# Summing the adaLN scale and shift vectors along the free dimension, and starting the first feed-forward layer one contraction tile at a time

## The chip, the cores and the metric

One core of a Trainium2 chip runs the whole program. The metric is the device time of one execution in microseconds (us); lower is better. The engines named below: TensorE (PE in the profile; PEld is its weight loads), VectorE (DVE), ScalarE (ACT), GpSimd (POOL), and SyncE (SP), which issues the DMA transfers.

## The reference: what is computed

A two-layer encoder on one sequence of 256 positions, width 1024, everything in float32. Each layer has three sub-layers (a feed-forward one, a mixer, a feed-forward one); layer 0's mixer is a gated MLP, layer 1's is banded attention. Every sub-layer is modulated by one vector `c`:

```
c_act = silu(c)                                        # (1, 1024)
mod   = (c_act @ w_ada[l] + b_ada[l]).reshape(9, 1024) # shift, scale, gate of 3 sub-layers
h = x * (1 + scale[i]) + shift[i]
y = swiglu(h, ffn_gu, ffn_down)                        # (silu(h @ Wg) * (h @ Wu)) @ Wd, d_ff = 2816
x = layer_norm(ALPHA * x + 0.5 * (1 + gate[i]) * y, ln_g, ln_b)
```

The shared keys and values of layer 1 have a scale and a shift of their own (`w_ada_kv`). So there are 20 vectors of 1024 numbers that are each a product of `c_act` with a 1024x1024 matrix: 14 scales and shifts, and 6 gates.

## The kernel before, in words

The 256 positions are two tiles (t = 0, 1) of 128 partitions. A large product takes a modulated, transposed activation tile (features on partitions) as the stationary operand and 512 weight columns as the moving one. For precision each operand is split into a rounded part `hi` and a remainder `lo` (fp32r): a product is three matmuls, `hi*hi`, `hi*lo`, `lo*hi` (L240, L241, L243, in `mm_unit`). A weight "unit" is a 128x1024 piece (512 KB): SP loads it into one of 6 `raw` buffers, ACT casts it to `hi` (L196), DVE subtracts to get `lo` (L197), and PE runs 12 matmuls on it (2 position tiles x 2 accumulators x 3).

A modulation vector is summed in `ada_slice`. The matrix is read in 8 pieces in which partition p holds row 8p+j; DVE multiplies piece j by the per-partition number `c_act[:, j]` and adds it to an accumulator `acc` (L114). After 8 pieces the sum over the 128 partitions remains. For a scale or shift (`finish_cols`) PE transposes the accumulator in 8 blocks of 128x128 (L129) and DVE reduces each half along its free dimension (L130), which leaves the vector with features on partitions. For a gate (`finish_gate`) PE multiplies by a matrix of ones instead. The pieces are fed in between the weight units: `ada_phase` lists the vectors of a phase with a number of units over which to spread them, and `pump`, called once for each unit, issues the next piece when enough credit has built up.

The first feed-forward layer starts cold, in `first_gu_part`. Its first part is two chunks of gate/up columns (512 and 256 wide). Scale and shift are summed for the first 512 features (8 pieces, L438), then `x` for these features is transposed on PE (L458), modulated on ACT (L294) and split; then matmuls on contraction tiles 0 to 3 run while the second 512 features go the same way. In this region the order on SP and PE is as written; elsewhere a scheduler sets the order of each engine's instructions at build time. Every engine works through its own queue in order.

After the first part come a down projection of these 768 columns, and then the other four chunks of 512 and their down projection (`PARTS2`).

Of the kernel before, what the change touches and what calls it, by code (L numbers as in the profile page):

```python
# [8 lines left out]
F32 = mybir.dt.float32  # L9
# [5 lines left out]
P = 128  # L15
D = 1024
# [28 lines left out]


@with_exitstack
def encoder_kernel(ctx, tc, a, out):
# [11 lines left out]
    accp = pool("accp", 2)  # L60
# [14 lines left out]

    c_raw = const.tile([P, KD], F32, name="c_raw")
    nc.sync.dma_start(out=c_raw, in_=a["c"])
    X = [xp.tile([P, D], F32, name=f"X{t}") for t in range(NT)]
    c_act = const.tile([P, KD], F32, name="c_act")
    nc.scalar.activation(c_act, c_raw, AF.Silu)  # L80
    ident = const.tile([P, P], F32, name="ident")
    make_identity(nc, ident)
    ones = const.tile([P, P], F32, name="ones")
# [12 lines left out]

    def load_small():
        small_dma(lncols, a["lncols"])
# [5 lines left out]
    def ada_slice(key, w_src, b_src, finish):  # L104
        st = {"acc": None}
# [15 lines left out]

    def finish_cols(key):
        def f(acc):
            m = modp.tile([P, KD], F32, tag="mod", name=nm("mod"))
            for half in range(2):
                tp = pt.tile([P, 512], F32, tag="pt", name=nm("adt"))
                for q in range(4):
                    j = half * 4 + q
                    nc.tensor.transpose(tp[:, q * P:(q + 1) * P], acc[:, j * P:(j + 1) * P], ident)  # L129
                nc.vector.reduce_sum(m[:, half * 4:half * 4 + 4],  # L130
                                     tp.rearrange("p (q n) -> p q n", q=4), axis=AX.X)
            mods[key] = m
        return f
# [17 lines left out]
    def mk_slice(key):  # L151
        if key[0] == "kv":
            n0 = key[1] * D
            wv = a["w_ada_kv"].rearrange("(p j) n -> p j n", j=KD)[:, :, n0:n0 + D]
            return ada_slice(key, wv, a["b_ada_kv"][:, n0:n0 + D], finish_cols(key))
        l, m = key
        n0 = m * D
        wv = a["w_ada"][l].rearrange("(p j) n -> p j n", j=KD)[:, :, n0:n0 + D]
        fin = finish_gate(key, 1.0 if m == 5 else 0.5) if m % 3 == 2 else finish_cols(key)
        return ada_slice(key, wv, a["b_ada"][l:l + 1, n0:n0 + D], fin)  # L160
# [149 lines left out]
    def affine(scl, shift, ln):  # L310

        A = modp.tile([P, KD], F32, tag="A", name=nm("A"))
        B = modp.tile([P, KD], F32, tag="B", name=nm("B"))
        if ln is None:
            nc.vector.tensor_scalar(A, scl, 1.0, None, op0=ALU.add)
            nc.vector.tensor_copy(B, shift)
        else:
            g, b = lncols[:, 0, ln, :], lncols[:, 1, ln, :]
            nc.vector.scalar_tensor_tensor(A, scl, 1.0, g, op0=ALU.add, op1=ALU.mult)
            nc.vector.scalar_tensor_tensor(B, scl, 1.0, b, op0=ALU.add, op1=ALU.mult)  # L320
            nc.vector.tensor_tensor(B, B, shift, op=ALU.add)
        return A, B
# [91 lines left out]
    def first_gu_part(w_gu, part, aT):  # L414

        units = [gu_units(w_gu, c0, wd) for c0, wd in part]
        accs = []
        wv = a["w_ada"][0].rearrange("(p j) (m n) -> p j m n", j=KD, m=9)[:, :, 0:2, :]
        bv = a["b_ada"][0:1, :].rearrange("o (m n) -> o m n", m=9)[:, 0:2, :]

        chunks = [(0, 1), (1, 1), (2, 2), (4, 2), (6, 2)]

        HK = KD // 2
        CW = HK * P
        sums = []
        for c in range(2):
            acc = accp.tile([P, 2, CW], F32, tag="acc", name=nm("acc"))
            nc.gpsimd.memset(acc, 0.0)
            nc.gpsimd.memset(acc[32:33, 1, :], 1.0)
            sums.append(acc)  # L430

        def products(c, js):
            for j in js:
                raw = unitp.tile([P, 2, CW], F32, tag=("hi", "lo")[j % 2], name=nm("raw"))
                nc.sync.dma_start(out=raw, in_=wv[:, j, :, c * CW:(c + 1) * CW])
                if j == 0:
                    nc.sync.dma_start(out=sums[c][0:1], in_=bv[:, :, c * CW:(c + 1) * CW])
                nc.vector.scalar_tensor_tensor(sums[c], raw, c_act[:, j:j + 1], sums[c],  # L438
                                               op0=ALU.mult, op1=ALU.add)

        def load_x(c):
            for t in range(NT):
                nc.sync.dma_start(out=X[t][:, c * CW:(c + 1) * CW],
                                  in_=a["x"][t * P:(t + 1) * P, c * CW:(c + 1) * CW])

        def modulate(c):
            m8 = modp.tile([P, 2, HK], F32, tag="m8", name=nm("m8"))
            for m in range(2):
                tp = pt.tile([P, 512], F32, tag="pt", name=nm("adt"))
                for q in range(HK):  # L450
                    nc.tensor.transpose(tp[:, q * P:(q + 1) * P], sums[c][:, m, q * P:(q + 1) * P], ident)
                nc.vector.reduce_sum(m8[:, m], tp.rearrange("p (q n) -> p q n", q=HK), axis=AX.X)
            for t in range(NT):
                p, tag = (ps, "ps") if c == 0 else (pt, "pt")
                tp = p.tile([P, 512], F32, tag=tag, name=nm("hp"))
                for q in range(HK):
                    k = c * HK + q
                    nc.tensor.transpose(tp[:, q * P:(q + 1) * P], X[t][:, k * P:(k + 1) * P], ident)  # L458
                hT[t].extend(modulated(tp, m8[:, 1], m8[:, 0], range(HK), htp, "h"))

        def load_units(k):

            for gi, uis in ((0, (k, k + 1)), (1, (k // 2,))):
                for ui in uis:
                    get(units[gi], ui)

        def matmuls(*todo):
            for gi, ui in todo:
                for t in range(NT):
                    mm_unit(accs[gi][t], hT[t], units[gi][ui], ui, KD)  # L470

        products(0, range(KD))
        load_x(0)
        modulate(0)
        accs.extend([new_accs(wd // 256) for _ in range(NT)] for _, wd in part)
        load_units(0)
        products(1, range(KD // 2))
        matmuls((0, 0), (0, 1), (1, 0))
        load_units(2)
        products(1, range(KD // 2, KD))  # L480
        load_x(1)
        matmuls((0, 2), (0, 3))
        modulate(1)
        matmuls((1, 1))
        load_units(4)
        load_units(6)
        matmuls((0, 4), (0, 5), (1, 2), (0, 6), (0, 7), (1, 3))
        for gi, (c0, wd) in enumerate(part):
            for t in range(NT):
                gu_out(t, accs[gi][t], wd, aT)  # L490
# [348 lines left out]
```

## Time and profile before

| | us |
|---|---|
| median of 3 runs | 1082.26 (1081.93 to 1084.04) |
| profiled execution | 1084.99 |
| its span in the profile | 1083.2 |
| PE busy | 1038.2 |
| DVE busy | 872.8 |
| ACT busy | 520.5 |

The profile comes from one execution. The span is what the profiler saw of it, the rest lies around it. "Busy" is the time in which at least one instruction of the engine is in flight. A matmul's own duration is longer than the distance to the next one, since they are pipelined; a run of matmuls is therefore read by their starts. In a row of the timeline, "[18.14 <-DVE acc L438]" means that the engine had been idle for 18.14 us and that the DVE instruction of line 438 on `acc` released it.

### The profile page before, as it was taken

How to read it: one execution, taken by the hardware profiler on the slowest of the kernel's cores; microseconds unless marked ns; L12 is line 12 of the kernel's file. 1: busy time of each engine (PE TensorE's matmuls, PEld its weight loads, DVE VectorE, ACT ScalarE, POOL GpSimd, SP SyncE). 2: the span in 40 equal slices, each digit the busy share in tenths (PEclk: the TensorE clock that was granted, in tenths of full speed). 3: DMA queues.
4: the chain of work that ended last, by engine and by line, in shares of the span. 5: the costliest groups of instructions: out<-in, count | busy, mean ns of one | idle time of the engine just before them, and what ended most of it. 6: DMA issues, size and time to landing. Idle time of an engine off the chain costs nothing. (4 is left out here: it accounts for less than half of the span.)

```text
span 1083.2 us, 13718 instructions
## 1 busy us (share of the span) xinstructions
PE 1038.2 (96%) x4888; PEld 853.3 (79%) x4888; DVE 872.8 (81%) x1095; ACT 520.5 (48%) x732; POOL 38.6 (4%) x55
## 2 busy tenths in 40 slices
PE   2899999999999999999999999999999999999996
PEld 1678888878777787888887888887887788888886
DVE  5889885689999999988779997758998869645635
ACT  3445553374345464443439554343748656445530
POOL 1000000000000010000000000000000000000000
PEclk9999999999999999999999999999999999999999
DMA  8988988659788778999876798768698837745621
GB/s 281 356 296 318 328 314 303 214 180 306 258 284 315 258 265 302 336 339 312 323 241 206 264 336 281 244 215 277 217 346 306 291 92 253 258 157 168 241 78 40
DMA packets 111809, 281.55 MB, mean 260 GB/s; under 512 B 9574, under 2 KB 22118, under 8 KB 111740
## 3 DMA queue, kind: packets, MB, share of 16 engines
q1 hardware_dynamic: 111740, 280.67, 74.8%
q8 instruction: 38, 0.62, 0.2%
q14 instruction: 31, 0.25, 0.1%
HBM read 279.58 MB, written 1.05 MB: 259 GB/s over the span
## 5 line engine op out<-in xcount | busy, mean ns | idle before, releaser
L196 ACT CAST hi<-raw 128x1024 fp32r<-128x1024 f32 x344 | 357.6, 1057 | 268.8 <-DMA raw<-ffn_gu 96.4
L197 DVE TENSOR_TENSOR lo<-raw,hi 128x1024 fp32r<-128x1024 f32 x344 | 413.8, 1219 | 55.3 <-ACT hi L196 49.1
L240 PE MATMUL acc<-hi,hh 128*128 128x512 f32 x928 | 365.8, 397 | 3.9 <-ACT hh L275 3.0
L241 PE MATMUL acc<-lo,hh 128*128 128x512 f32 x928 | 361.0, 392 | 1.6 <-DVE lo L197 1.5
L243 PE MATMUL acc<-hi,hl 128*128 128x512 f32 x928 | 293.3, 391 | 0.0
L240 PEld LDWEIGHTS acc<-hi,hh 128*128 128x128 f32 x928 | 174.9, 189 | 40.9 <-ACT hh L275 4.4
L241 PEld LDWEIGHTS acc<-lo,hh 128*128 128x128 f32 x928 | 175.1, 189 | 37.5 <-DVE lo L197 3.2
L243 PEld LDWEIGHTS acc<-hi,hl 128*128 128x128 f32 x928 | 174.6, 188 | 36.8
L114 DVE SCALAR_TENSOR_TENSOR acc<-raw,c_act,acc 128x1024 f32<-128x1024 f32 x144 | 184.1, 1278 | 16.3 <-DMA raw<-w_ada 16.0
L240 PE MATMUL acc<-hi,th 128*128 128x512 f32 (+1 forms) x432 | 165.2, 388 | 0.5 <-ACT th L275 0.2
L241 PE MATMUL acc<-lo,th 128*128 128x512 f32 (+1 forms) x432 | 163.4, 384 | 1.0 <-DVE lo L197 0.9
L243 PE MATMUL acc<-hi,tl 128*128 128x512 f32 (+1 forms) x432 | 143.4, 383 | 0.0
L241 PEld LDWEIGHTS acc<-lo,th 128*128 128x128 f32 x432 | 80.9, 188 | 17.4 <-DVE lo L197 2.9
L240 PEld LDWEIGHTS acc<-hi,th 128*128 128x128 f32 x432 | 81.2, 188 | 16.3 <-ACT th L275 0.9
L243 PEld LDWEIGHTS acc<-hi,tl 128*128 128x128 f32 x432 | 80.5, 188 | 15.7
L403 ACT ACTIVATE sg<-acc 128x512 f32<-128x512 f32 (+1 forms) x48 | 27.1, 564 | 90.1 <-PE acc L243 89.6
L404 DVE TENSOR_TENSOR a<-acc,sg 128x512 f32<-128x512 f32 (+1 forms) x48 | 30.9, 643 | 47.9 <-ACT sg L403 47.9
L276 DVE TENSOR_TENSOR tl<-tp,th 128x512 fp32r<-128x512 f32 (+1 forms) x56 | 36.0, 648 | 38.3 <-ACT th L275 38.3
L275 ACT CAST th<-tp 128x512 fp32r<-128x512 f32 (+1 forms) x56 | 30.9, 556 | 73.3 <-PE tp L282 73.1
L294 ACT ACTIVATE hf<-hp,B,A 128x128 f32<-128x128 f32 x96 | 36.6, 474 | 58.7 <-PE hp L306 42.8
L334 DVE TENSOR_TENSOR gy<-acc,gate 128x512 f32<-128x512 f32 (+1 forms) x49 | 32.0, 673 | 17.8 <-PE acc L243 17.8
L110 POOL MEMSET acc<- 128x1024 f32 x18 | 17.2, 956 | 604.7 <-PE adt L129 429.2
(99 smaller groups left out, 593.6 us busy)
## 6 DMA issues: line engine op xcount, KB each, us to landing
raw<-ffn_gu SPq DMA_DIRECT2D x160, 512.0 KB, 5.9
raw<-w_ada SPq DMA_DIRECT2D x144, 512.0 KB, 5.1
raw<-ffn_down SPq DMA_DIRECT2D x88, 512.0 KB, 4.9
raw<-w_in SPq DMA_DIRECT2D x32, 512.0 KB, 6.0
raw<-ffn_gu SPq DMA_DIRECT2D x32, 256.0 KB, 4.7
raw<-w_out SPq DMA_DIRECT2D x16, 512.0 KB, 6.0
raw<-w_ada_kv SPq DMA_DIRECT2D x16, 512.0 KB, 5.2
raw<-w_kv SPq DMA_DIRECT2D x16, 512.0 KB, 5.7
```

The lines of the kernel that those rows point to most:

```text
L114: nc.vector.scalar_tensor_tensor(st["acc"], raw, c_act[:, j:j + 1], st["acc"], op0=ALU.mult, op1=ALU.add)
L196: nc.scalar.copy(hi, raw)
L197: last["lo"] = eng.tensor_tensor(lo, raw, hi.bitcast(F32), op=ALU.subtract)
L240: nc.tensor.matmul(acc, lhsT=xh, rhs=wh[:, sl], start=k == 0, stop=False)
L241: nc.tensor.matmul(acc, lhsT=xh, rhs=wl[:, sl], start=False, stop=False)
L243: nc.tensor.matmul(acc, lhsT=xl, rhs=wh[:, sl], start=False, stop=k == nk - 1)
L275: nc.scalar.copy(hi, src_ps)
L276: nc.vector.tensor_tensor(lo, src_ps, hi.bitcast(F32), op=ALU.subtract)
L294: nc.scalar.activation(hf[:, sl], tp[:, sl], AF.Identity, bias=B[:, j:j + 1], scale=A[:, j:j + 1])
L334: nc.vector.tensor_tensor(tmp, acc[:, :c1 - c0], g[:, sl], op=ALU.mult)
L403: nc.scalar.activation(sg[:, :wd], g, AF.Silu)
L404: nc.vector.tensor_tensor(av[:, :wd], u, sg[:, :wd], op=ALU.mult)
```

## The change

Three things change together.

1. The 14 scale and shift matrices are handed over transposed (`w_cols`, features in rows), 128 features a piece. `c_act` is spread over all partitions once (`c_row`), and one DVE instruction (`tensor_tensor_reduce`) multiplies a piece by it and sums along the free dimension, straight into the column of the result. The bias is its start value; 1 has been added to the biases of the scales, so that `affine` no longer adds it. PE's transposes and DVE's reductions of `finish_cols` go. Gates are summed as before, from `w_gate`, with one accumulator buffer in place of two.
2. The first part of the first feed-forward layer takes its first two chunks (512 and 512 columns) one contraction tile k at a time: 128 features of scale and of shift, `x` for these features (handed over transposed, `xT`), then one weight unit of each chunk. PE first runs 48 transposes of the identity into a tile that nothing reads. `x` itself is loaded later.
3. The first layer's parts are (512, 512, 512) and (512, 512, 256); a down projection takes its short piece first. Its gate is spread over 13 units, the next scale and shift over 24.

```diff
+COLS = [(0, 1), (0, 0), (0, 4), (0, 3), (0, 7), (0, 6), (1, 1), (1, 0), ("kv", 1), ("kv", 0),
+        (1, 4), (1, 3), (1, 7), (1, 6)]
...
+    def column(ci, j, m, raw=None):
+        if raw is None:
+            raw = rawp.tile([P, D], F32, tag="raw", name=nm("raw"))
+            nc.sync.dma_start(out=raw, in_=a["w_cols"][ci, j * P:(j + 1) * P, :])
+        nc.vector.tensor_tensor_reduce(out=raw, in0=raw, in1=c_row, scale=1.0,
+                                       scalar=bcol[:, ci, j:j + 1], op0=ALU.mult, op1=ALU.add,
+                                       accum_out=m[:, j:j + 1])
...
-    def finish_cols(key):
-        def f(acc):
-            m = modp.tile([P, KD], F32, tag="mod", name=nm("mod"))
-            for half in range(2):
-                tp = pt.tile([P, 512], F32, tag="pt", name=nm("adt"))
-                for q in range(4):
-                    j = half * 4 + q
-                    nc.tensor.transpose(tp[:, q * P:(q + 1) * P], acc[:, j * P:(j + 1) * P], ident)
-                nc.vector.reduce_sum(m[:, half * 4:half * 4 + 4],
-                                     tp.rearrange("p (q n) -> p q n", q=4), axis=AX.X)
-            mods[key] = m
-        return f
...
     def first_gu_part(w_gu, part, aT):
...
+        warm = pt.tile([P, 512], F32, tag="pt", name=nm("warm"))
+        for i in range(N_WARM):
+            nc.tensor.transpose(warm[:, i % 4 * P:(i % 4 + 1) * P], ident, ident)
...
+        for k in range(KD):
+            raws = []
+            for ci in range(2):
+                raw = rawp.tile([P, D], F32, tag="raw", name=nm("raw"))
+                nc.sync.dma_start(out=raw, in_=a["w_cols"][ci, k * P:(k + 1) * P, :])
+                raws.append(raw)
+                if k + ci == 0:
+                    load_first()
+            if k % 2 == 0:
+                half = slice(k % 4 * SEQ, (k % 4 + 2) * SEQ)
+                nc.sync.dma_start(out=xT[k // 4][:, half], in_=a["xT"][:, k // 4, half])
+            for ci, m in enumerate((sc, sh)):
+                column(ci, k, m, raws[ci])
+            if second:
+                matmuls(1, k - 1, second())
+            hf, (hi, lo) = tiles(k)
+            nc.scalar.activation(hf, xT[k // 4][:, k % 4 * SEQ:(k % 4 + 1) * SEQ], AF.Identity,
+                                 bias=sh[:, k:k + 1], scale=sc[:, k:k + 1])
+            split4(hf, (hi, lo))
+            matmuls(0, k, halves(units[0][k])())
+            second = halves(units[1][k])
+        for t in range(NT):
+            gu_out(t, accs[0][t], 512, aT)
+        matmuls(1, KD - 1, second())
+        for t in range(NT):
+            gu_out(t, accs[1][t], 512, aT)
...
-        for k0 in range(0, nk, KD):
-            n = min(KD, nk - k0)
+        cut = [0, *range(nk % KD or KD, nk + 1, KD)]
+        for k0, k1 in zip(cut, cut[1:]):
+            n = k1 - k0
...
-                with tc.manual_schedule(engines={ET.SP, ET.PE}):
-                    first_gu_part(w_gu, part, aT)
+                with tc.manual_schedule(engines={ET.SP, ET.PE, ET.DVE, ET.Activation}):
+                    first_gu_part(w_gu, part[:2], aT)
                 start()
+                gu_part(w_gu, part[2:], aT)
+                load_small()
...
-        start=lambda: (load_small(), ada_phase(([(0, 2)], 5), ([(0, 4), (0, 3)], 40))))
+        start=lambda: (load_c(), ada_phase(([(0, 2)], 13), ([(0, 4), (0, 3)], 24))))
```

`halves` loads a unit and issues ACT's cast at once; the function that it returns issues DVE's subtraction. `tiles` gives the tiles for `h` of contraction tile k, for both position tiles together (128x256).

The order on PE from the program's start, before (`adt` takes the transposed sums, `hp` the transposed `x`, `acc` the products):

```order
L451 MATMUL adt_160<-ident,acc_126 128x128 x4
L451 MATMUL adt_166<-ident,acc_126 128x128 x4
L458 MATMUL hp_172<-ident,X_102 128x128 x4
L458 MATMUL hp_186<-ident,X_103 128x128 x4
L240 MATMUL acc_200<-hi_208,hh_182 128x512
L241 MATMUL acc_200<-lo_209,hh_182 128x512
```

and now:

```order
L440 MATMUL warm_128<-ident 128x128 x48
L263 MATMUL acc_177<-hi_206,hh_199 128x512
L264 MATMUL acc_177<-lo_207,hh_199 128x512
L263 MATMUL acc_178<-hi_206,hh_199 128x512
L264 MATMUL acc_178<-lo_207,hh_199 128x512
```

The transposes of the sums and of `x` have left the way to the first product, and 48 transposes that wait for nothing but the identity stand ahead of it.

The order on DVE in the first layer's first part now, from its last contraction tile (k = 7) into the next chunk (L129 is the new sum and the read of its result, L471 and L220 a unit's `lo`, L299 the remainder of `h`, L424 the product of gate and up; buffer numbers kept):

```order
L129 ISA raw_82_509,mod_10_185<-raw_82_509,c_row_100,bcol_106 128x1024
L129 ISA mod_10_185 128x1
L129 ISA raw_83_511,mod_11_186<-raw_83_511,c_row_100,bcol_106 128x1024
L129 ISA mod_11_186 128x1
L471 TENSOR_TENSOR lo_81_507<-raw_79_504,hi_80_506 128x1024
L299 TENSOR_TENSOR hl_75_482<-hf_73_480,hh_74_481 128x256
L471 TENSOR_TENSOR lo_86_534<-raw_84_531,hi_85_533 128x1024
L424 TENSOR_TENSOR a_91_555<-acc_3_178,sg_90_554 128x512
L424 TENSOR_TENSOR a_93_559<-acc_5_180,sg_92_558 128x512
L471 TENSOR_TENSOR lo_89_552<-raw_87_549,hi_88_551 128x1024
L220 TENSOR_TENSOR lo_102_591<-raw_100_588,hi_101_590 128x1024
```

The second chunk's last `lo` (lo_89) stands behind the two products a_91 and a_93, which need the first chunk's finished accumulators.

Where a scale vector was finished in the middle of the program, PE had before (in the first layer's second part):

```order
L243 MATMUL acc_223_1071<-hi_251_1168,hl_59_354 128x512
L243 MATMUL acc_224_1072<-hi_251_1168,hl_59_354 128x512
L129 MATMUL adt_254_1179<-ident_106,acc_151_731 128x128 x4
L129 MATMUL adt_255_1185<-ident_106,acc_151_731 128x128 x4
L240 MATMUL acc_223_1071<-hi_257_1193,hh_59_354 128x512
L241 MATMUL acc_223_1071<-lo_258_1194,hh_59_354 128x512
```

and now (in the same part) one unit's products follow those of the unit before:

```order
L266 MATMUL acc_289_1397<-hi_281_1368,hl_75_482 128x512
L266 MATMUL acc_290_1398<-hi_281_1368,hl_75_482 128x512
L263 MATMUL acc_289_1397<-hi_284_1380,hh_74_481 128x512
L264 MATMUL acc_289_1397<-lo_285_1381,hh_74_481 128x512
L263 MATMUL acc_290_1398<-hi_284_1380,hh_74_481 128x512
```

Eight transposes have gone from between two units; there were twelve such places.

## Rows read from the trace of the kernel before

**Rows 1.** The page's part 1: busy us, share of the span, instructions.
```profile
PE 1038.2 (96%) x4888; PEld 853.3 (79%) x4888; DVE 872.8 (81%) x1095; ACT 520.5 (48%) x732; POOL 38.6 (4%) x55
```

**Rows 2.** Waits of PE: waiter <- releaser: total us, times, longest.
```profile
PE adt L451 <- DVE acc L438: 18.1, 1, 18.1
...
PE acc L240 <- ACT hh L275: 3.0, 1, 3.0
```

**Rows 3.** Timeline, first 40 us: start us, length us, engine, line, operation.
```profile
1.86 0.29 POOL masks.py:199 TENSOR_SCALAR_AFFINE_SELECT ident<-ident 128x128 f32<-128x128 f32 x1
...
5.24 1.28 DVE L438 SCALAR_TENSOR_TENSOR acc<-raw,c_act,acc 128x1024 f32<-128x1024 f32 x1 [3.34 <-DMA raw<-w_ada]
...
8.66 9.37 DVE L438 SCALAR_TENSOR_TENSOR acc<-raw,c_act,acc 128x1024 f32<-128x1024 f32 x7 [2.14 <-DMA raw<-w_ada]
...
18.14 1.94 PE L451 MATMUL adt<-ident,acc 128*128 128x128 f32 x8 [18.14 <-DVE acc L438]
...
24.79 0.55 PE L240 MATMUL acc<-hi,hh 128*128 128x512 f32 x1 [3.02 <-ACT hh L275]
```

**Rows 4.** Timeline of PE where the first two chunks end.
```profile
66.91 1.03 PE L282 MATMUL tp<-ident,a 128*128 128x128 f32 x8
```

**Rows 5.** Stretches: length, busy us of each engine (instructions), PE clock, DMA share, GB/s.
```profile
0.00:10.00 10.00, 0.00 (x0) 0.00 (x0) 3.64 (x8) 1.49 (x2) 3.57 (x10) 1.00 0.68 216
10.00:20.00 10.00, 1.86 (x9) 1.90 (x10) 8.39 (x7) 0.62 (x1) 0.00 (x0) 1.00 1.05 387
20.00:30.00 10.00, 6.99 (x24) 5.24 (x23) 6.85 (x8) 6.34 (x13) 0.96 (x1) 0.83 0.78 252
```

**Rows 6.** The page's part 6: a DMA issue, count, size, median us to landing.
```profile
raw<-w_ada SPq DMA_DIRECT2D x144, 512.0 KB, 5.1
```

**Rows 7.** Groups by line and shape: busy us, mean ns | idle before.
```profile
L197 DVE TENSOR_TENSOR lo<-raw,hi 128x1024 fp32r<-128x1024 f32 x344 | 413.8, 1219 | 55.3 <-ACT hi L196 49.1
L196 ACT CAST hi<-raw 128x1024 fp32r<-128x1024 f32 x344 | 357.6, 1057 | 268.8 <-DMA raw<-ffn_gu 96.4 <-PE acc L243 77.5 <-DMA raw<-w_in 33.9
...
L114 DVE SCALAR_TENSOR_TENSOR acc<-raw,c_act,acc 128x1024 f32<-128x1024 f32 x144 | 184.1, 1278 | 16.3 <-DMA raw<-w_ada 16.0
...
L404 DVE TENSOR_TENSOR a<-acc,sg 128x512 f32<-128x512 f32 x40 | 27.5, 688 | 47.4 <-ACT sg L403 47.4
...
L403 ACT ACTIVATE sg<-acc 128x512 f32<-128x512 f32 x40 | 24.0, 599 | 84.1 <-PE acc L243 83.7
...
L130 DVE TENSOR_REDUCE mod<-adt 128x4 f32<-128x512 f32 x24 | 15.6, 683 | 3.0 <-PE adt L129 2.9
...
L677 DVE CUSTOM_DVE_ANT_0 pr<-sc,bias 128x256 f32<-128x256 f32 x16 | 6.4, 417 | 1.9 <-POOL bias L666 1.8 <-issue 0.2
...
L677 DVE CUSTOM_DVE_ANT_0 pr<-sc,bias 128x128 f32<-128x128 f32 x16 | 3.8, 286 | 1.4 <-POOL bias L666 1.0 <-PE sc L673 0.4
...
L276 DVE TENSOR_TENSOR tl<-tp,th 128x256 fp32r<-128x256 f32 x8 | 3.3, 419 | 3.1 <-ACT th L275 3.1
...
L403 ACT ACTIVATE sg<-acc 128x256 f32<-128x256 f32 x8 | 3.1, 386 | 5.9 <-PE acc L243 5.9
...
L677 DVE DVE_READ_ACCUMULATOR2_ANT m<- 128x1 f32 x32 | 2.7, 83 | 0.0
```

**Rows 8.** Timeline of PE around the end of one scale vector.
```profile
141.39 0.62 PE L243 MATMUL acc<-hi,hl 128*128 128x512 f32 x2
141.84 1.03 PE L129 MATMUL adt<-ident,acc 128*128 128x128 f32 x8
142.63 0.47 PE L240 MATMUL acc<-hi,hh 128*128 128x512 f32 x1
142.95 0.39 PE L241 MATMUL acc<-lo,hh 128*128 128x512 f32 x1
```

**Rows 9.** Two long stretches in the middle, columns as in rows 5.
```profile
220.00:420.00 200.00, 195.51 (x891) 158.46 (x890) 189.41 (x241) 102.43 (x142) 9.87 (x11) 1.00 0.79 268
420.00:620.00 200.00, 198.78 (x920) 163.83 (x919) 174.18 (x195) 100.61 (x138) 6.73 (x7) 1.00 0.83 291
```

More of the change, by code (lines that the diff above doesn't have):

```diff
@@ L73, in nm @@
         return f"{s}_{uid[0]}"
+    c_row = const.tile([P, D], F32, name="c_row")
+    nc.sync.dma_start(out=c_row, in_=a["c"].partition_broadcast(P))
+    X = [xp.tile([P, D], F32, name=f"X{t}") for t in range(NT)]
     c_raw = const.tile([P, KD], F32, name="c_raw")
[L77 to L78 removed]
     c_act = const.tile([P, KD], F32, name="c_act")
[L80 removed]
+    bcol = const.tile([P, len(COLS), KD], F32, name="bcol")
     ident = const.tile([P, P], F32, name="ident")
     make_identity(nc, ident)
+    nc.scalar.activation(c_row, c_row, AF.Silu)
     ones = const.tile([P, P], F32, name="ones")
@@ L101, in load_small, with col_slice, step, gate_slice @@
         nc.gpsimd.memset(wsT[CH:P, :, 0:CH], 0.0)
-    def ada_slice(key, w_src, b_src, finish):
-        st = {"acc": None}
+    def column(ci, j, m, raw=None):
[5 more added lines that the diff above has]
+                                       accum_out=m[:, j:j + 1])
+    def col_slice(key):
+        ci = COLS.index(key)
+        st = {}
+        def step(j):
+            if j == 0:
+                st["m"] = modp.tile([P, KD], F32, tag="mod", name=nm("mod"))
+            column(ci, j, st["m"])
+            if j == KD - 1:
+                mods[key] = st["m"]
+        return [lambda j=j: step(j) for j in range(KD)]
+    def gate_slice(key):
+        w_src = a["w_gate"][key[0] * 3 + key[1] // 3].rearrange("(p j) n -> p j n", j=KD)
+        b_src = a["b_gate"][key[0] * 3 + key[1] // 3][None, :]
+        finish = finish_gate(key, 1.0 if key[1] == 5 else 0.5)
+        st = {}
         def step(j):
@@ L432, in products @@
[L432 to L439, printed above, removed]
@@ L461, in load_units @@
[L461 to L476, printed above, removed]
@@ new lines, in matmuls, with halves, second @@
+        def matmuls(gi, k, w):
+            for t in range(NT):
+                mm_unit(accs[gi][t], hT[t], w, k, KD)
+        def halves(srcs):
+            raw = load_raw(srcs)
+            hi = unitp.tile([P, D], F32R, tag="hi", name=nm("hi"))
+            lo = unitp.tile([P, D], F32R, tag="lo", name=nm("lo"))
+            nc.scalar.copy(hi, raw)
+            def second():
+                last["lo"] = nc.vector.tensor_tensor(lo, raw, hi.bitcast(F32), op=ALU.subtract)
+                return hi, lo
+            return second
```

104 lines of the change are left out of this document (40 added, 64 removed).

## The prediction

> **What bounds the kernel now.** I read the page's busy shares first, then the waits of PE, then the timelines of the places that the diff touches. The shares say that PE is the bound: it is busy for 1038.2 us, 96% of the span, and DVE comes next with 872.8 us [rows 1]. The waits of PE say where the rest is: one wait of 18.1 us for the first sums on DVE and one of 3.0 us for the first modulated tile, both before the first product [rows 2]. So an edit pays if it starts PE earlier or takes instructions from PE, and only there. It loses if DVE, which has no large reserve, gets longer work.
>
> The timeline of the start shows the two waits in place: DVE sums eight pieces until 18.03 us, PE transposes until 21.8 us, and the first product starts at 24.79 us, after 3.02 us of idle [rows 3]. The first part's two chunks are done at 66.91 us, where PE goes on to transposing their output [rows 4]. By then PE has worked off 12 units (8 of the 512-wide chunk, 4 of the 256-wide one).
>
> **The unit prices.** Two 512-column matmuls start 0.45 us apart in sum (141.39 to 141.84) [rows 8], so one takes 0.225 us and a unit of 12 takes 2.7 us of PE. A unit costs ACT 1.06 us and DVE 1.22 us [rows 7]. The first ten microseconds move 216 GB/s, the next ten 387 GB/s [rows 5]; a 512 KB piece (0.524 MB [rows 6]) takes 1.35 us at the second rate.
>
> The new sum is not in the trace in its form, but the same instruction with the same read of its result is, on attention scores: 286 ns for 128 elements, 417 ns for 256, and 83 ns for the read [rows 7]. That is 1.02 ns an element, so 0.417 + 768 x 0.00102 = 1.20 us for 1024, and 1.28 us with the read. The instruction that it replaces takes 1.28 us too [rows 7]: I count the swap at nothing. But those scores come from PSUM on one side, while here both inputs lie in SBUF, so the price has another end, worked out under the rivals.
>
> [...] The old multiply-and-add with two float32 inputs in SBUF runs at full rate in this trace, which leaves the form with an accumulated result open: no row here shows it.
>
> **The start, step by step.** Before the first product the new kernel loads the spread `c` (0.52 MB), the first scale piece (0.52), the biases (0.06), the first shift piece (0.52), a quarter of `x` (0.26) and the first unit (0.52): 2.4 MB. Before, the first piece landed at 5.24 us and the second by 8.66 us [rows 3]; I give the spread `c` the first of these times. ACT then passes over it (1.06 us, price of a cast of that size), which the second load hides. First sum about 8.0 to 9.3; the second piece lands about 9.4, so second sum to 10.7. ACT modulates and rounds 128x256 (0.39 us each, by the 256-wide row [rows 7]) to 11.5, casts the unit to 12.6, DVE makes `lo` to 13.8. The first product is at about 12.6 us instead of 24.79, and the second, which needs `lo`, at 13.8.
>
> The 48 warm-up transposes can start when the identity is there, at 2.15 us [rows 3]. PE's first eight transposes took 1.94 us [rows 3], eight later ones 1.03 us [rows 8], so 48 take 6.2 to 11.6 us and end between 8.4 and 13.8. They cost nothing or, at worst, 1.2 us.
>
> From then on each contraction tile k is one round: DVE 2 x 1.28 + 2 x 1.22 + 0.42 (remainder of `h`, 256 wide [rows 7]) = 5.4 us; PE 24 x 0.225 = 5.4 us; DMA four pieces and an eighth of `x` a round, 2.23 MB, at 387 GB/s 5.8 us. Three engines are nearly equal, and I take the longest, 5.8. The lower end is 5.4. The upper end comes from the buffers: six raw buffers hold one and a half rounds, and the next shift piece may be issued only when the buffer of the last round's second unit is free, that is after this round's second sum (1.28) and that unit's `lo` (1.22). With the 5.1 us that a piece takes from issue to landing [rows 6], which includes queueing, a round is 7.6 us. I keep 5.8, since a load that finds the queue nearly empty should take much less than that median.
>
> Last `lo` of the first chunk: 13.8 + 7 x 5.8 = 54.4 us. Eleven products remain: 56.9. Now comes the added wait: the second chunk's last `lo` stands on DVE behind the two gate-times-up products, and these need ACT's silu of the finished accumulators. Silu 0.60, product 0.69, `lo` 1.22 [rows 7] and 0.3 for the last product to come out: 2.8 us, to 59.7, then eleven products, 62.2 us. PE fills a part of it: four products of the next chunk stand in between (0.9 us of work done ahead).
>
> At 62.2 us PE has done 16 units and those four products, against 12 units at 66.91 us. The gain is 66.91 - 62.2 = 4.7, plus 4 x 2.7 = 10.8, plus 0.9: 16.4 us. I take off 1.4 us for the chunk that follows, which starts with no weights prepared ahead: over it DVE has eight `lo`, five gate pieces, four splits and two products, 8 x 1.22 + 5 x 1.28 + 6 x 0.69 = 20.3 us against 21.6 us of PE, close to even; it could also cost 5. **Start: 15.0 us**, between 2 (rounds of 7.6 take 12.6 off) and 19 (rounds of 5.4 and no loss after).
>
> If PE's clock falls in the wait of 2 to 3 us at the end of the first part, as it did after the idle 3.0 us before (0.83 of full speed on average over 20 to 30 us [rows 5]), the eleven products cost up to 2.5 us more; this lies inside that range.
>
> **The rest of the program.** Twelve vectors are finished without PE. Eight transposes delayed the second product after them from 141.84 + 0.225 = 142.07 to 142.95 [rows 8], 0.88 us, on an engine that is the bound. **12 x 0.88 = 10.6 us.** DVE loses 24 reductions of 0.683 us, 16.4 us [rows 7], which is worth 0 to 3 us, since between 220 and 420 us DVE is 95% busy and PE idles for 4.5 us [rows 9]; I take 0. The sums' loads are as large as before. `x` (1 MB, now read twice) and the small constants move behind the third chunk on SP's queue; they are wanted at the end of the down projection, some 30 us later, and cost nothing. One accumulator in place of two: the next gate begins a whole sub-layer later, nothing. The first layer's other 24 units and the reordered chunks have the same number of products, nothing.
>
> **Sum.** 15.0 + 10.6 = 25.6 us. The profiled execution took 1084.99 us, so it would be 1059.4; it was 2.7 us above the median of 1082.26, so the median would be 1056.7. I predict 1057.
>
> **The rivals.**
> - *The sum runs at half rate* and the kernel gets slower. Each of 112 sums then costs 1024 x 0.00102 = 1.05 us more of DVE. In the start DVE's round is 7.5 us in place of 5.8: 7 x 1.7 = 12 us. In the gated MLP (220 to 420 us) 16 sums add 16.8 and four reductions less give back 2.7, against 10.6 us of reserve [rows 9]: 3.5 to 14 us. In the second feed-forward layer (about 420 to 620 us) 32 sums add 28 net against 25.8 of reserve: 2 to 28 us. Middle of both together 24, in sum 36: 1093 us. It decides from about 1.95 us a sum on, where the loss eats the 25.6. For it: no row with this form. Against it: full rate with one input in PSUM.
> - *The loads bound the start*: rounds of 7.6 us through the chain over raw buffers. Then 12.6 us less: 1069 us. For it: the chain is closed, and loads took 5.1 us. Against it: that median was taken with more loads in flight.
> - *PE gets its transposes back as waits*: it was held by late `lo` anyway, and only the start pays: 1082.3 - 15.0 = 1067 us. For it: DVE at 95% [rows 9]. Against it: DVE is relieved at the same places, and all idle time of PE is only 4% of the span [rows 1].
> - *Both of the last two*, so that the change does next to nothing of what it says: 1080 us.
>
> **How the numbers follow.** Forecast 0.60 (its own range 1050 to 1064), slow loads 0.15, waits in place of transposes 0.10, both 0.05, half rate 0.10. The range of 1049 to 1073 takes in the first three and leaves out the last two. What a measurement of this kernel can tell from no change is about 0.2%, 2.2 us. Faster by more: 0.60 + 0.15 + 0.10 + most of 0.05, 0.88; within it 0.02; slower 0.10.
>
> **What would show it.** In the profile after: the group of the new sum at 1.20 us (2.25 would be the half rate); the first real product at 12 to 14 us; rounds of 5.8 us between the `lo` of the first chunk, and what each waits for (DVE busy through: the sums; a wait for `w_cols`: the loads); the first part's last product near 62 us, with one gap of about 2 us before it; no more transposes of sums; PE's share of the span at 97 to 98%. The prediction is wrong if the stretch from 70 us to the end shrinks by clearly less than 10 us net of the four units done earlier, or if rounds are above 7 us.

## The result, and the profile after

| | before | after |
|---|---|---|
| time, median (range) | 1082.63 us (1081.93 to 1084.04, 4 runs) | 1058.11 us (1057.66 to 1060.1, 4 runs) |
| ratio | 1 | 0.9775 [0.9759, 0.9792] |
| profiled execution | 1084.99 us | 1058.18 us, span 1056.4 us |

The change gains 24.5 us, or about 2.3%; forecast were 1057 us and a gain of 25.6. The page's first part, to be set beside [rows 1]:

```profile
PE 1031.2 (98%) x4808; PEld 844.2 (80%) x4808; DVE 856.9 (81%) x1184; ACT 519.8 (49%) x729; POOL 24.3 (2%) x39
```

PE's share has risen from 96 to 98%, as forecast. DVE has lost 16 us of work and keeps its 81%. The waits of PE, columns as in [rows 2]; the 18.1 us for the first sums are gone:

```profile
PE hp L329 <- DVE X L378: 4.5, 6, 2.1
PE acc L264 <- DVE lo L220: 3.1, 3, 1.7
PE acc L264 <- DVE lo L471: 2.8, 6, 0.9
```

All that is left of waiting is small, and most of it is for DVE. The groups by line and shape show the new sum, which no row of before had in this form:

```profile
L220 DVE TENSOR_TENSOR lo<-raw,hi 128x1024 fp32r<-128x1024 f32 x328 | 395.0, 1220 | 53.7 <-ACT hi L219 48.0
L129 DVE CUSTOM_DVE_ANT_0 raw<-raw,c_row,bcol 128x1024 f32<-128x1024 f32 x112 | 142.9, 1278 | 8.8 <-DMA raw<-w_cols 8.4
L158 DVE SCALAR_TENSOR_TENSOR acc<-raw,c_act,acc 128x1024 f32<-128x1024 f32 x48 | 61.4, 1279 | 6.5 <-DMA raw<-w_gate 6.3
```

It takes 1278 ns with both inputs in SBUF, the same as the multiply-and-add that it replaces (1279 here, 1278 before [rows 7]). The half rate, on which the slower rival stood, would have shown about 2.25 us by the prediction's estimate (1.20 + 1.05).

The timeline of PE at the start, columns as in [rows 3]:

```profile
2.21 8.31 PE L440 MATMUL warm<-ident 128*128 128x128 f32 x48 [2.21 <-POOL ident masks.py:199]
11.85 0.50 PE L263 MATMUL acc<-hi,hh 128*128 128x512 f32 x1 [1.33 <-ACT hi L468]
13.11 0.50 PE L264 MATMUL acc<-lo,hh 128*128 128x512 f32 x1 [0.76 <-DVE lo L471]
```

The first real product comes at 11.85 us instead of 24.79, the second at 13.11. The warm-up transposes end at 10.52, ahead of both. One round on DVE, from the first chunk's `lo` of one contraction tile to that of the next (same columns):

```profile
11.83 1.23 DVE L471 TENSOR_TENSOR lo<-raw,hi 128x1024 fp32r<-128x1024 f32 x1 [0.52 <-ACT hi L468]
13.22 1.28 DVE L129 CUSTOM_DVE_ANT_0 raw<-raw,c_row,bcol 128x1024 f32<-128x1024 f32 x1 [0.17 <-DMA raw<-w_cols]
14.44 0.08 DVE L129 DVE_READ_ACCUMULATOR2_ANT mod<- 128x1 f32 x1
14.51 1.28 DVE L129 CUSTOM_DVE_ANT_0 raw<-raw,c_row,bcol 128x1024 f32<-128x1024 f32 x1
...
15.72 1.22 DVE L471 TENSOR_TENSOR lo<-raw,hi 128x1024 fp32r<-128x1024 f32 x1
16.91 0.43 DVE L299 TENSOR_TENSOR hl<-hf,hh 128x256 fp32r<-128x256 f32 x1
17.86 1.23 DVE L471 TENSOR_TENSOR lo<-raw,hi 128x1024 fp32r<-128x1024 f32 x1 [0.52 <-ACT hi L468]
```

DVE is busy through, but for 0.52 us that it waits for ACT's cast and, in some rounds, 0.1 to 0.2 us for a load. Where nothing is waited for, the sums start 1.21 us apart (7.28 and 8.49 us), read included: a row's end overlaps the next row's start. The eight of these `lo` start at 11.83, 17.86, ... 52.98: 41.15 / 7 = 5.88 us a round. The end of the first part on PE:

```profile
57.46 1.20 PE L263 MATMUL acc<-hi,hh 128*128 128x512 f32 x4
58.89 0.50 PE L263 MATMUL acc<-hi,hh 128*128 128x512 f32 x1 [0.22 <-DVE a L424]
60.02 0.50 PE L264 MATMUL acc<-lo,hh 128*128 128x512 f32 x1 [0.63 <-DVE lo L471]
...
62.20 0.62 PE L266 MATMUL acc<-hi,hl 128*128 128x512 f32 x2
62.65 0.61 PE L264 MATMUL acc<-lo,hh 128*128 128x512 f32 x2
...
65.38 0.81 PE L305 MATMUL tp<-ident,a 128*128 128x128 f32 x6
```

Sixteen units and four products of the next chunk are done at 62.65 us; 62.2 was worked out. The two gaps shown, before the second chunk's last products, sum to 0.85 us, not 2. PE's granted clock also differs: in before it was 0.83 from 20 to 30 us [rows 5] and again from 40 to 50 us, in after 1.00 in every stretch of ten from 0 to 80 us. What part of the gain that is, no run separates.

**The rest, from sub-layer to sub-layer.** PE's first transposes of a new sub-layer's activations mark its beginning: at 219.23, 373.40, 565.02, 757.80, 880.00 and (last product) 1074.97 us in before, at 200.87, 355.42, 542.21, 733.64, 853.61 and 1048.64 after. The lead is 18.4 us at the first mark, 18.0 at the second, then 22.8, 24.2, 26.4 and 26.3. The stretches between them, of before and then of after (columns as in [rows 5]). The gated MLP's row and the sum are shown:

```profile
219.23:373.40 154.17, 150.43 (x683) 122.00 (x684) 144.99 (x188) 74.35 (x98) 6.84 (x7) 1.00 0.79 271
...
sum 855.74, PE 845.64 PEld 695.68 DVE 698.91 ACT 426.33 POOL 28.18; mean PE 169.13 PEld 139.14 DVE 139.78 ACT 85.27 POOL 5.64
```
```profile
200.87:355.42 154.55, 149.76 (x678) 122.18 (x676) 147.08 (x204) 76.94 (x100) 6.09 (x6) 1.00 0.82 283
...
sum 847.77, PE 837.74 PEld 688.40 DVE 689.60 ACT 426.71 POOL 19.71; mean PE 167.55 PEld 137.68 DVE 137.92 ACT 85.34 POOL 3.94
```

From the first mark on, PE is busy 845.64 - 837.74 = 7.9 us less and the stretch is 855.74 - 847.77 = 8.0 us shorter. Ten of the twelve vectors lie in it, forecast were 8.8. In the gated MLP, where two of the ten lie, nothing is gained: DVE is busy for 147.1 of 154.6 us, and PE's idle time rises from 3.7 to 4.8 us. In the second feed-forward layer, where four lie, the stretch is 4.8 us shorter.

### The profile page after: what moved, and what is told of

Its sections match the earlier page's. It is cut to its first block, busy times and chain, and to the rows that moved or that the text cites. A ratio compares the mean times of both kernels' runs of the same rounds, so it can differ in the third digit from the quotient of the medians.

```text
span 1056.4 us, 13554 instructions
## 1 busy us (share of the span) xinstructions
PE 1031.2 (98%) x4808; PEld 844.2 (80%) x4808; DVE 856.9 (81%) x1184; ACT 519.8 (49%) x729; POOL 24.3 (2%) x39
## 3 DMA queue, kind: packets, MB, share of 16 engines
HBM read 281.16 MB, written 1.05 MB: 267 GB/s over the span
## 5 line engine op out<-in xcount | busy, mean ns | idle before, releaser
L219 ACT CAST hi<-raw 128x1024 fp32r<-128x1024 f32 x328 | 341.5, 1057 | 217.4 <-DMA raw<-ffn_gu 64.2
L220 DVE TENSOR_TENSOR lo<-raw,hi 128x1024 fp32r<-128x1024 f32 x328 | 395.0, 1220 | 53.7 <-ACT hi L219 48.0
L263 PE MATMUL acc<-hi,hh 128*128 128x512 f32 x928 | 360.1, 395 | 2.0 <-ACT hi L468 1.3
L129 DVE CUSTOM_DVE_ANT_0 raw<-raw,c_row,bcol 128x1024 f32<-128x1024 f32 x112 | 142.9, 1278 | 8.8 <-DMA raw<-w_cols 8.4
L424 DVE TENSOR_TENSOR a<-acc,sg 128x512 f32<-128x512 f32 (+1 forms) x48 | 30.9, 643 | 48.1 <-ACT sg L423 48.1
L158 DVE SCALAR_TENSOR_TENSOR acc<-raw,c_act,acc 128x1024 f32<-128x1024 f32 x48 | 61.4, 1279 | 6.5 <-DMA raw<-w_gate 6.3
L299 DVE TENSOR_TENSOR tl<-tp,th 128x512 fp32r<-128x512 f32 (+1 forms) x56 | 36.4, 649 | 31.6 <-ACT th L298 31.5
```

The source lines that it names most:

```text
L129: nc.vector.tensor_tensor_reduce(out=raw, in0=raw, in1=c_row, scale=1.0, scalar=bcol[:, ci, j:j + 1], op0=ALU.mult, op1=ALU.add, accum_out ...
L158: nc.vector.scalar_tensor_tensor(st["acc"], raw, c_act[:, j:j + 1], st["acc"], op0=ALU.mult, op1=ALU.add)
L219: nc.scalar.copy(hi, raw)
L220: last["lo"] = eng.tensor_tensor(lo, raw, hi.bitcast(F32), op=ALU.subtract)
L263: nc.tensor.matmul(acc, lhsT=xh, rhs=wh[:, sl], start=k == 0, stop=False)
L299: nc.vector.tensor_tensor(lo, src_ps, hi.bitcast(F32), op=ALU.subtract)
```

## The experiments

Each kernel was run beside the kernel before on the same chip. The medians of before were 1082.86 us beside E1, E2, E4 and E9, 1083.8 beside E3, E5, E6 and E7, and 1081.67 beside E10 to E12. "After" is the changed kernel; ratios are to before, with their 95% intervals.

**E1, one part alone: the sums of the twelve later vectors, with the old start.**

```diff
-    accp = pool("accp", 2)
+    accp = pool("accp", 1)
...
     def mk_slice(key):
-        if key[0] == "kv":
-            n0 = key[1] * D
-            wv = a["w_ada_kv"].rearrange("(p j) n -> p j n", j=KD)[:, :, n0:n0 + D]
-            return ada_slice(key, wv, a["b_ada_kv"][:, n0:n0 + D], finish_cols(key))
+        if key in COLS:
+            return col_slice(key)
```

> The kernel before with one part of the change: the twelve scale and shift vectors after the first sub-layer are summed along the free dimension; the start and the first layer's parts stay as before. Theory (PE is the bound, so its transposes are paid in full): 10.6 us less than before, 1072 us, within 1069 to 1075. Rival (PE was held by late weight units anyway, so the transposes come back as waits): 1080 to 1083 us. Rival (the start gave all): no change.

Measured: 1075.74 us (1074.46 to 1076.49), ratio 0.9931 [0.991, 0.9951]: -7.1 us, just short of the range expected; by the interval the gain is 5.3 to 9.7 us. Its marks give the stretch from the first one to the end, cut in five (only the sum row is shown):

```profile
sum 847.97, PE 836.75 PEld 687.18 DVE 687.11 ACT 426.44 POOL 19.87; mean PE 167.35 PEld 137.44 DVE 137.42 ACT 85.29 POOL 3.97
```

Against before, PE is busy for 8.9 us less, 0.89 a vector, as priced; the stretch is 7.8 us shorter. So 1.1 us came back as waits. PE's waits in the gated MLP of this kernel, from 218.43 to 373.60 us, show the place (in before this line was 1.8 us in its gated MLP):

```profile
PE hp L321 <- DVE X L369: 3.5, 3, 1.7
```

**E2, the other part alone: the new start, with the later vectors through transposes as before.**

```diff
-COLS = [(0, 1), (0, 0), (0, 4), (0, 3), (0, 7), (0, 6), (1, 1), (1, 0), ("kv", 1), ("kv", 0),
-        (1, 4), (1, 3), (1, 7), (1, 6)]
+COLS = [(0, 1), (0, 0)]
...
-    accp = pool("accp", 1)
+    accp = pool("accp", 2)
...
+    def finish_cols(key):
```

> The changed kernel with only its start, its parts and its pacing: the twelve later vectors are again summed on DVE, transposed on PE and reduced, with two accumulators. Theory: the start alone is worth 16.6 us (the first sub-layer's last transposes came 18.4 us earlier, of which two vectors are 1.8), so 1066 us, within 1063 to 1069. Rival (the two parts help each other: the transposes cost more once PE has less idle time): above 1069. Rival (the denser pacing of the first layer gives part of it back): above 1069 as well, with the loss before 200 us.

Measured: 1066.13 us (1064.91 to 1072.18), ratio 0.9854 [0.982, 0.9889]: -16.7 us; by the interval 12.0 to 19.5, wide because of one run at 1072.18. By the medians the two parts add up: 16.7 + 7.1 = 23.8 of 24.5.

**E9, the transposes alone, put back without the sums' reductions.** After each later vector PE transposes the identity eight times, and nobody reads the result.

```diff
+    def blocks():
+        for half in range(2):
+            tp = pt.tile([P, 512], F32, tag="pt", name=nm("adt"))
+            for q in range(4):
+                nc.tensor.transpose(tp[:, q * P:(q + 1) * P], ident, ident)
...
             if j == KD - 1:
                 mods[key] = st["m"]
+                after(LAG_M, blocks)
```

> The changed kernel with eight transposes of the identity put back on PE after each of the twelve later vectors; no reduction on DVE, nothing waits for them. Theory (PE's time alone is what the twelve places were worth): 12 x 0.88 = 10.6 us more, 1068.7 us, within 1066 to 1071. Rival (the gain after the start came from the 16.4 us that DVE lost in reductions): 1058 to 1061 us.

Measured: 1068.79 us (1065.93 to 1069.43), ratio 0.987 [0.9846, 0.9893], 10.7 us above after by the medians. The span of its profiled execution is 7.8 us above that of after. So PE's time for eight transposes is worth 0.65 to 0.89 us of the total a vector. The interval lies wholly above that of after, and DVE has none of its reductions back: the rival, that the gain came from DVE's relief, falls.

**E4, the sums' DVE time doubled**: the 96 later sums are each issued twice, the second time into a spare column.

```diff
+        again = raw is None
...
+        if again:
+            twice = smp.tile([P, 1], F32, tag="twice", name=nm("twice"))
+            nc.vector.tensor_tensor_reduce(out=raw, in0=raw, in1=c_row, scale=1.0,
+                                           scalar=bcol[:, ci, j:j + 1], op0=ALU.mult, op1=ALU.add,
+                                           accum_out=twice)
```

> The changed kernel with every one of the 96 later sums issued twice on DVE, the second into a number that nothing reads; the start is unchanged. This puts 96 x 1.28 = 123 us more on DVE and asks what a sum at half rate would have cost. By the prediction's way of counting (reserve of DVE in each stretch of the changed kernel: 10 us between 200 and 400 us against 20 added, 28 between 400 and 600 against 41, 36 between 600 and 800 against some 25) at least 23 us more, and up to 50 because DVE's reserve is not where it is needed: 1081 to 1108 us, 1093 as the middle. Rival (DVE works ahead of PE far enough that only the overflow counts): 1075 to 1082 us. Rival (PE hides it all): 1058 to 1063 us.

Measured: 1116.11 us (1114.8 to 1119.93), ratio 1.031 [1.0282, 1.0339], 58 us above after, and outside what was expected. The page's busy times by stretch (columns as in [rows 5]) and PE's first wait:

```profile
200.00:400.00 200.00, 181.87 (x796) 143.79 (x794) 191.02 (x270) 87.89 (x122) 7.57 (x9) 0.98 0.76 253
400.00:600.00 200.00, 191.80 (x838) 152.28 (x839) 195.27 (x270) 91.70 (x117) 1.56 (x3) 0.99 0.81 275
600.00:800.00 200.00, 196.16 (x895) 160.49 (x893) 181.49 (x232) 100.79 (x138) 5.21 (x5) 1.00 0.77 264
800.00:900.00 100.00, 91.24 (x472) 72.44 (x471) 95.44 (x227) 56.38 (x125) 2.42 (x10) 0.93 0.80 260
...
sum 1115.00, PE 1053.13 PEld 848.84 DVE 966.18 ACT 520.55 POOL 23.81; mean PE 175.52 PEld 141.47 DVE 161.03 ACT 86.76 POOL 3.97
```
```profile
PE acc L271 <- DVE lo L227: 24.9, 29, 2.9
```

DVE gets 109 us more, and the total rises by 58. Between 200 and 600 us and in attention (800 to 900 us, which I had left out) DVE is busy for 95 to 98% of the time and PE for less; between 600 and 800 us, where sums run too, PE stays the busier one (98%). PE executes the same 4808 instructions and yet is busy for 22 us longer. Its granted clock was 0.983 on average over the span (0.997 in after) and 0.93 from 800 to 900 us: PE, which was made to wait for `lo` for 24.9 us (3.1 in after), also had the lower clock here. By these two averages the clock makes at most some 16 of the 22 us, an estimate: 0.017 x 1113 less 0.003 x 1056. Had the half rate been true, the loss would have been larger than the rival's 36 us: its 96 x 1.05 = 101 us of later DVE time at this rate (58 / 109) would cost some 54 us by this estimate, in place of the 24 that I gave the later stages.

**E3, without the warm-up transposes.**

```diff
-N_WARM = 48
+N_WARM = 0
```

> The changed kernel without the 48 transposes of the identity. Theory (the first rounds are paced by DVE and the loads, so a low clock on PE's first products is caught up by PE's 0.4 us of idle time a round): 0 to 2 us more, 1058 to 1060 us. Rival (each round's wait keeps the clock low, so that a round takes twice 5.4 us of PE): rounds near 11 us, 1080 us and more.

Measured: 1058.17 us (1056.75 to 1059.67), ratio 0.9763 [0.9746, 0.9781]: no difference. PE's first products in its timeline:

```profile
11.61 0.80 PE L263 MATMUL acc<-hi,hh 128*128 128x512 f32 x1 [11.61 <-ACT hi L465]
12.87 0.80 PE L264 MATMUL acc<-lo,hh 128*128 128x512 f32 x1 [0.46 <-DVE lo L468]
13.47 0.63 PE L263 MATMUL acc<-hi,hh 128*128 128x512 f32 x1
13.89 0.63 PE L264 MATMUL acc<-lo,hh 128*128 128x512 f32 x1
...
17.73 0.39 PE L263 MATMUL acc<-hi,hh 128*128 128x512 f32 x1
```

For the first 6 us the products start 0.42 us apart, afterwards 0.23, after 11.6 us without work. The profile's granted clock reads 1.00 from 10 to 20 us, so the cause is not shown. In before the same spacing stands with a low reading: the products that start at 25.56, 25.99 and 26.42 us are 0.43 apart, and from 26 to 28 us the granted clock is 0.50. A lower clock in E3 would fit that, but no reading of E3 shows one. The wider spacing costs nothing in the total (1058.17 us against 1058.11): a round takes 5.9 us and PE's work in it 5.4 [rows 8], so PE catches up.

**E5, the cast of the first chunk's unit ahead of the modulation**, so that DVE no longer waits 0.52 us for ACT.

```diff
+            first = halves(units[0][k])
             hf, (hi, lo) = tiles(k)
 ...
-            matmuls(0, k, halves(units[0][k])())
+            matmuls(0, k, first())
```

> The changed kernel with ACT's cast of the first chunk's unit placed ahead of the modulation of x, so that DVE no longer waits 0.52 us in each round for that cast. Theory (a round is DVE's chain of two sums, lo, remainder, wait for the cast, lo: 5.88 us): the round falls to about 5.4 us, 7 x 0.45 = 3 us less, 1055 us. Rival (loads at 387 GB/s set the round at 5.76): 0.8 us less, 1057 us. Rival (the cast's unit has not landed by then and holds up the modulation behind it): longer rounds, 1058 to 1062 us.

Measured: 1061.44 us (1059.5 to 1062.37), ratio 0.9791 [0.9774, 0.9809]: 3 us above after by the medians, with intervals that overlap; the 3 us forecast as a gain are not there. ACT's timeline:

```profile
22.54 1.05 ACT L468 CAST hi<-raw 128x1024 fp32r<-128x1024 f32 x1 [4.04 <-DMA raw<-ffn_gu]
23.50 0.59 ACT L493 ACTIVATE hf<-xT,mod,mod 128x256 f32<-128x256 f32 x1
```

The unit's load is later than the sums. With the cast in front, ACT stands 4 us at that load, and the modulation queues behind it though its sums are done. The first chunk's `lo` now start 6.09 us apart on average (12.65 to 55.25 us), and the first part ends 2.4 us later than in after. The loads thus follow closely behind DVE: in this order they bind, with waits of ACT of 2.27 to 4.68 us for a load between 15 and 40 us. Why they are late is not separated: up to 55 us SP's issues for `w_cols` wait 11.7 us (10.0 in after) until a `lo` has freed its raw buffer, and E5 with eight raw buffers was not run.

**E6, eight raw buffers** in place of six (ten of `hi` and `lo` each in place of eleven).

```diff
-N_RAW = 6
-N_UNIT = 11
+N_RAW = 8
+N_UNIT = 10
```

> The changed kernel with eight raw buffers in place of six, paid for with ten weight-unit buffers in place of eleven. Theory (the round is DVE's chain, loads wait for buffers but not on the path): rounds stay at 5.7 to 5.9 us, only the 0.2 us waits for w_cols in some rounds go, first product of the ninth unit pair unchanged within 1 us. Rival (the chain over the raw buffers sets the round): rounds fall to 5.4 us or below. The total also holds what the lost unit buffer costs later, so the rounds are what is read.

Measured: 1057.63 us (1057.08 to 1058.76), ratio 0.9758 [0.9742, 0.9775]: not to be told from after. Two `lo` in DVE's timeline:

```profile
18.01 1.23 DVE L471 TENSOR_TENSOR lo<-raw,hi 128x1024 fp32r<-128x1024 f32 x1 [0.52 <-ACT hi L468]
...
23.71 1.22 DVE L471 TENSOR_TENSOR lo<-raw,hi 128x1024 fp32r<-128x1024 f32 x1 [0.52 <-ACT hi L468]
```

The waits for `w_cols` are gone from these rounds and a round is 23.71 - 18.01 = 5.70 us; the loads added no more than 0.18 us to it. ACT's timeline in between shows what closes it:

```profile
21.69 0.60 ACT L492 ACTIVATE hf<-xT,mod,mod 128x256 f32<-128x256 f32 x1 [2.75 <-DVE mod L129]
22.32 0.41 ACT L298 CAST hh<-hf 128x256 fp32r<-128x256 f32 x1
22.64 1.99 ACT L468 CAST hi<-raw 128x1024 fp32r<-128x1024 f32 x2
```

The modulation waits for the second sum, and the next `lo` for the cast behind it. So the round is a loop over two engines: 3.68 us on DVE (first chunk's `lo` and two sums, 18.01 to 21.69) and 2.02 us on ACT (modulation, rounding, cast, 21.69 to 23.71). DVE's other `lo` and the remainder run beside ACT, with 0.52 us to spare. By these rows a shorter `lo` or remainder there would leave the round as it is; no run tests that.

**E7: E5, and the second chunk's last `lo` ahead of the two gate-times-up products.**

```diff
+        last_unit = second()
         for t in range(NT):
             gu_out(t, accs[0][t], 512, aT)
-        matmuls(1, KD - 1, second())
+        matmuls(1, KD - 1, last_unit)
```

> As the kernel with the cast first, and with the second chunk's last lo placed on DVE ahead of the two products of gate and up. Theory: the 0.85 us that PE waits at the end of the first part go as well, 0.9 us less than the kernel with the cast first, 1054 us. Rival (the wait moves to the next chunk, whose first units are late then): the same as the kernel with the cast first.

Measured: 1059.41 us (1056.42 to 1067.29), ratio 0.9781 [0.9754, 0.9808]: some 2 us below E5, not below after. The intervals overlap, so it settles nothing about the order of `lo` alone.

**E10, the gate at the end of the gated MLP begun later.** In after PE waits 2.05 us for the normalised activations at 353.37 us. DVE's timeline of after there:

```profile
349.67 0.20 DVE L369 BATCH_NORM_AGGREGATE mv<-st 128x2 f32<-128x12 f32 x1
351.80 1.29 DVE L158 SCALAR_TENSOR_TENSOR acc<-raw,c_act,acc 128x1024 f32<-128x1024 f32 x1 [1.93 <-DMA raw<-w_gate]
353.00 0.15 DVE L371 TENSOR_SCALAR rs<-mv 128x1 f32<-128x1 f32 x1
```

A gate piece that waits for its load stands on the queue between two steps of the normalisation. PE's granted clock falls after this wait, to 0.56 from 356 to 358 us (row of ten us below, columns as in [rows 5]); the eight products between 356.84 and 359.76 us start up to 0.43 us apart in place of 0.23:

```profile
350.00:360.00 10.00, 7.95 (x33) 6.26 (x32) 6.39 (x9) 7.91 (x14) 1.70 (x2) 0.83 0.86 277
```

```diff
     ada_phase(([(0, 8)], 11), ([(1, 1), (1, 0), ("kv", 1), ("kv", 0)], 44))
+    ada["steps"][:8] = [(4.0 if i == 0 else 1.0, s) for i, (_, s) in enumerate(ada["steps"][:8])]
```

> The kernel after, with one edit: the first piece of the gate that is begun at the end of the gated MLP comes 4 units into the next sub-layer instead of 1.4, the other seven one unit apart, done after 11 units as before. Theory (the 2.05 us for which PE waits at 353.37 us of the kernel after are the price of a gate piece that waits 1.93 us for its load on DVE's queue ahead of the normalisation): that wait of PE falls below 0.6 us, the first transposes of the next sub-layer come 1 to 2 us sooner (before 354.4 us in a profile with the same start), total 1056 to 1057.5. Rival (the normalisation is late for the whole queue of DVE's work there, not for the one piece): PE still waits 1.5 us or more at that place, total 1058 to 1060.

Measured: 1058.33 us (1055.48 to 1062.53), ratio 0.9778 [0.9755, 0.9802]: the total did not move by the medians, though the interval is too wide to rule out the 0.6 to 2.1 us forecast. The wait itself did, in PE's timeline (three rows of it):

```profile
351.92 0.63 PE L329 MATMUL hp<-ident,X 128*128 128x128 f32 x4 [0.21 <-DVE X L378]
...
416.65 0.50 PE L264 MATMUL acc<-lo,hh 128*128 128x512 f32 x1 [0.40 <-DVE lo L220]
...
422.47 0.49 PE L264 MATMUL acc<-lo,hh 128*128 128x512 f32 x1 [0.68 <-DVE lo L220]
```

A third such wait of 0.45 us stands between the last two rows. From 340 to 545 us PE's waits sum to 2.35 us here and to 2.51 in after. The wait for the normalisation fell from 2.05 to 0.21, and 1.5 us of waits for `lo` came 65 us later, where DVE was busy for all of 410 to 420 us. The clock did not fall either: it is 1.00 from 350 to 360 us. Counted by the first product of the new sub-layer (356.74 us here, 359.76 in after) 3.0 us are gained, and at the next mark 0.1 is left (542.08 against 542.21), more given back than the sums of waits show. My theory took the place of the wait for its cause. The rival's number for the total came true but not its wait. This one profile suggests that what binds here is the amount of DVE's work over the stretch, and that the order chooses where PE pays for it; no run takes DVE work away to test that.

**E11: E6, and the second chunk's last `lo` first (the edit of E7 without that of E5).**

> The kernel after with 8 raw buffers and 10 buffers each for hi and lo, and with the second chunk's last lo issued ahead of the two gate-times-up products of the first chunk. Theory (the first part is set by DVE's chain of 5.70 us a round and at its end by the products ahead of lo): the gap of PE before the last product goes (0.6 us), first part done 1.2 to 2 us sooner than 62.65; total 1055.5 to 1057. Rival (what is gained there is given back by the next chunk, which then waits for DVE): total 1057 to 1059, not to be told from the kernel after.

Measured: 1055.78 us (1053.5 to 1056.46), ratio 0.9749 [0.973, 0.9769]. By the medians it is 2.3 us below after and the best of all, but the interval overlaps with that of after. PE's timeline at the end of the first part:

```profile
62.09 0.62 PE L263 MATMUL acc<-hi,hh 128*128 128x512 f32 x2
62.55 0.60 PE L305 MATMUL tp<-ident,a 128*128 128x128 f32 x4
```

No gap is left, and PE reaches these transposes at 62.55 us against 65.38 after. At the first mark it leads after by 3.5 us, at the third by 2.3, at the fourth by 0.7, at the fifth by 1.9, and its span is 2.4 us shorter; the total lies in its theory's range. A part of the gain is given back as waits for `lo`, the line that was 3.1 us in after. E6 has 6.6 us on that line, also with ten unit buffers in place of eleven, so the missing buffer may be the reason; no run separates it:

```profile
PE acc L264 <- DVE lo L220: 7.5, 7, 2.9
```

**E12: E10 and E11 together.**

> The edits of the last two together. If both pay: 1054 to 1056. If neither does: 1057 to 1059.

Measured: 1056.34 us (1055.34 to 1057.58), ratio 0.9758 [0.9739, 0.9777]: between its two expectations and not better than E11. The later gate adds nothing here that the runs could show.

## Why the prediction was right, step by step

The total and its two sources came out: an earlier start, and PE's time for the transposes. Inside the sum two steps were wrong, and one term is not settled.

- **The sum of the start (15.0 us)** measured 16.7 alone (E2, 12.0 to 19.5 by its interval). The first product was 0.75 us earlier than worked out: the first sum starts at 7.28 us, not at 8.0.
- **The round (5.8 us)** measured 5.88, but for another reason. I let DMA set it. A loop of DVE and ACT does (E6): DVE's own work, two sums with their reads, two `lo` and the remainder, is 5.2 us as they start one after the other, and 0.52 us of waiting for ACT closes it at 5.70. My own DVE figure of 5.4 had no wait in it, and I had priced the modulation of a tile with that of a silu of the same width, 0.39 us [rows 7]; with scale and bias by partition it takes 0.60. The loads give 371 to 399 GB/s between 10 and 50 us, near the 387 used, and come next (E5, E6). That the number held is luck: two causes of nearly the same size.
- **The chain over raw buffers** (rounds of 7.6 us) fell for the order that was built: with six buffers loads cost under 0.2 us a round. In E5's order the loads do bind.
- **The end of the first part (62.2 us)** measured 62.65; the added wait was 0.85 us instead of about 2. PE was still working off products when the last `lo` came due. The granted clock is 1.00 from 50 to 70 us.
- **The allowance of 1.4 us for the next chunk** was not needed. By the count of the prediction the lead at 62.65 us is 4.3 + 10.8 + 0.9 = 16.0 us; at the first mark it is 18.4, or 16.6 without two vectors at 0.88. Between the two points PE waits for only 0.7 us. This is why the start gave more than 15.0.
- **The twelve vectors (10.6 us)**: the price per vector holds (0.89 us of PE in E1), the worth to the total is measured unevenly: 7.1 us in E1, 8.0 by E2 against after, 9.7 by the marks (26.3 less 16.6), 10.7 by E9's median and 7.8 by its profile. Only E1's interval, 5.3 to 9.7, leaves the 10.6 out. So the term is right or up to a third too large. The sign set for it held: from 62.65 us to the end the lead grows from 16.0 to 26.3 us, 10.3 net. In E1, 1.1 us of it came back as waits; in after the gated MLP, where DVE runs at 95%, gives nothing: there the rival of the waits was right, for one stage out of five.
- **DVE's relief, taken at 0**, was right. DVE loses 9.3 us of work from the first mark on, and the stretch is shorter by 8.0 us, about the 7.9 by which PE is less busy; E9 takes the gain back with PE's transposes alone.
- **The half rate** fell on one row (1278 ns a sum; 1200 was worked out, and 2250 for the half rate). It was a supposition, and no run shows it: E4's sums took 1278 and 1276 ns. Its price was too low, as far as E4's doubled sums stand for it.
- By the medians the start was 1.7 us too small and the vectors as much as 3.5 too large: the errors cancel in part, so the total, 1.1 us off, is nearer than its terms, and that too is luck.

## What to carry to other kernels

Count time taken from the bound engine in full only where the second engine has room. Here the transposes of four vectors, taken from PE, made the second feed-forward layer 4.8 us shorter, beside DVE busy for 163.2 of 186.8 us (87%); those of two made the gated MLP no shorter, beside DVE at 95%. A wait that is moved out of one place can show up later: in E10 one went from 2.05 to 0.21 us, and 1.5 us of others came 65 us on. So compare a whole stretch, by the sum of waits and by marks at its ends, and not the one wait that went: the sum leaves out what a lower clock after a wait costs (0.83 from 350 to 360 us of after). When two or three engines agree within 10% in a loop, name the one that sets it only after adding the waits between them into its chain.

## What the runs showed of the hardware

- A sum with an accumulated result over two float32 inputs in SBUF took 1278 ns for 128x1024 on average of 112 instances (1216 to 1287), the multiply-and-add of the gates 1279 ns for the same shape; from one sum's start to the next, with its read, it was 1.21 us where nothing was waited for.
- An activation with scale and bias by partition took 602 ns for 128x256, against 406 for a cast of the same shape.
- After 11.6 us without work, PE's first products started 0.42 us apart for some 6 us (E3); with 48 transposes ahead of them they started 0.23 us apart from the third on. The total was the same.
- After a wait of 2.05 us (353.37 to 355.42 us of after) PE's granted clock was 0.83 from 350 to 360 us, and its products started up to 0.43 us apart until 359.40 us; in E10, where the wait was 0.21 us, the clock was 1.00 there and they started 0.23 apart.
